# Head of a 15-product matmul kernel: whole-row loads, float16 casts ahead of TensorE's transposes, tile 9 by a transfer

## The chip, the core and the metric

The kernel runs on one core of one Trainium2 chip. The metric is device time in microseconds (us) of one execution; lower is better.

## What is computed

Two matrix products share x; the tanh of the one multiplies the other.

```python
batch, m, k, n = 16, 512, 1024, 768          # x: (16, 512, 1024), w1 and w2: (1024, 768), float32

def reference(x, w1, w2):
    y1 = np.matmul(x, w1)
    y2 = np.matmul(x, w2)
    return (np.tanh(y1) * y2).astype(np.float32)
```

x has 8192 rows, that is 64 tiles of 128 rows; k is eight blocks of 128.

## The kernel before

**Tiles.** All products run in float16 with sums in PSUM. The 2 x 768 output columns are taken as three blocks of 512: `a` is w1's first 512, `b` is w2's first 512, and `G` is the last 256 columns of w1 beside the last 256 of w2. Tiles 0 to 3 (the head) are multiplied in the plain way: for each tile and block one matmul of 128x512 for each of the eight k. Tiles 4 to 63 go in 20 triples. A triple would need 3 tiles x 3 blocks x 8 matmuls; a fast scheme needs 15 products of four matmuls each (`C_OPS`), on sums of x blocks (`A_SUMS`, made by VectorE for each triple, line 506), on sums of w blocks (`B_SUMS`, 11 of them, made once by VectorE at line 496), and on sums of the results (ScalarE copies and VectorE adds). In all there are 88 plain matmuls, 8 for tile 3's block `b` that is held back to the very end (in 16 halves), and 20 x 15 x 4 in the triples: 1296 matmuls of 512 columns.

**Getting operands.** w arrives as float32 in pieces that SP's queue loads in the order of the table `SP_LOADS` (two on ScalarE's queue, `ACT_LOADS`): `a3` is block a of k = 3 (128 rows of 2 KB), `g2` and `h2` are the 256 last columns of w1 and w2 for k = 2 and 3 (256 rows of 1 KB). Each piece is 256 KB and is cast by ScalarE (line 436) or VectorE (line 438) into the float16 array `wh`, whose columns stand in the order a, g, h, b. Head tiles of x come as float32 in halves of 256 KB (`x2.0` is tile 2, k = 0 to 3); TensorE transposes the float32 itself (line 456), and the way out of PSUM casts to float16. Later tiles are loaded by POOL's queue (line 472), which casts on the way. Tiles 4, 5, 6 and 9 (`POOL_LOADS`) are then transposed by TensorE in float16 (line 464), all others by a DMA transpose on SP's queue (line 475). `5.0:a4` means that POOL waits (a one-column copy of `a4`, line 585) until a4 has landed, and then loads tile 5's first half and the entries that follow. ScalarE also sums |x| and |w| for a range check (line 478).

**Order.** Nothing is left to the hardware to order: a planner in the kernel (`Planner`) simulates the engines from a table of costs, due times and margins (`MARGIN`, `MUL_DUE`), and every engine's queue is written in the order of its start times. `PE_HEAD` gives the order of half blocks (`2a0`: tile 2, block a, k = 0 to 3) and of the first triple's products for due times in the head. `WARM` and `FILLERS` are matmuls of a constant (line 850) whose result is unused: three at the start, and others ahead of the operation that is named. Queues run in order, so a late operation holds up all behind it.

Of the kernel before, what the change touches and what calls it, by code (L numbers as in the profile page):

```python
# [78 lines left out]
PE_HEAD = ("0G1 2a0 1G1 0a1 1a1 2b1 2G0 1G0 0b0 p10 0a0 0b1 p7 p6 p12 2G1 "  # L79
           "p9 3G1 p1 1a0 p11 3a1 2a1 0G0 2b0 3G0 p14 1b1 1b0 3a0 p8")  # L80
# [5 lines left out]
MUL_DUE = 0.200  # L86
MARGIN = {"S": 0.773, "B": 0.080, "T": 5.87, "L": 9.71, "early": 0.024}
# [3 lines left out]
FILLERS = {"PT0.1": (256,)}  # L91
# [4 lines left out]
EARLY_LOADS = {0: 0.35}  # L96
# [235 lines left out]
def kernel(  # L332
# [7 lines left out]
    nc = tc.nc  # L340
    P = 128
# [10 lines left out]
    XH_BUFS, XT_BUFS, S_BUFS, O_BUFS, C_BUFS, WF_BUFS = 7, 3, 2, 4, 2, 12  # L352
    D_SLACK, T_SLACK = 10.68, 1.17
    S_SOON, S_FROM, D_FROM, D_EARLY = 6.65, 2, 8, 2.87
    SPLIT = 5
    PACE, STORES, ST_HEAD, ST3G = "4544", (1.56, 2.37, 3.04), (12, 17, 19), 100
    sp_loads = [("Lx" if n[0] == "x" else "L") + n.lstrip("x") for n in SP_LOADS.split()]
    act_loads = ["L" + n for n in ACT_LOADS.split()]
    y_tiles = {int(n[1]) for n in SP_LOADS.split() if n[0] == "y"}
    x32_tiles = {int(n[1]) for n in SP_LOADS.split() if n[0] == "x"}  # L360
    XF_BUFS, XG_BUFS = max(len(x32_tiles), 1), max(HEAD - len(x32_tiles), 1)
# [50 lines left out]
    def load_x32(e, mt, h):  # L412
        if mt not in x32:
            x32[mt] = xfpool.tile([P, K], f32, tag="xf", name="x_f")
        pin(nc.sync.dma_start(x32[mt][:, h * F:(h + 1) * F], xf[mt][:, h * F:(h + 1) * F]))  # L415

    def load_y(e, mt, h):
        wfs[mt, h] = wfpool.tile([P, F], f32, tag="wf", name="w_f")
        pin(nc.sync.dma_start(wfs[mt, h], xf[mt][:, h * F:(h + 1) * F]))

    def cast_y(e, mt, h):
        if mt not in xhs:
            xhs[mt] = xgpool.tile([P, K], f16, tag="xh", name="xh")
        copy(e, xhs[mt][:, h * F:(h + 1) * F], wfs[mt, h])

    def load_w(e, c, k):

        wfs[c, k] = wfpool.tile([P, F], f32, tag="wf", name="w_f")
        if c in "ab":
            pin(engine[e].dma_start(wfs[c, k], wr["ab".index(c)][:, k, :F]))  # L430
        else:
            pin(engine[e].dma_start(wfs[c, k].rearrange("p (k n) -> p k n", k=2), wr["gh".index(c)][:, k:k + 2, F:]))
# [7 lines left out]
    COLUMNS = {"a": 0, "g": F, "h": N, "b": 2 * F}  # L440

    def cast_w(e, c, k):
        lo = COLUMNS[c]
        if c in "ab":
            copy(e, wh[:, k, lo:lo + F], wfs[c, k])
        else:
            copy(e, wh[:, k:k + 2, lo:lo + G], wfs[c, k].rearrange("p (k n) -> p k n", k=2))
# [32 lines left out]
    def abs_x(e, mt):  # L480
        abs_sum(e, x32[mt] if mt in x32 else xhs[mt], mt)
# [4 lines left out]
    def w_block(v):  # L486
        if v in wsum:
            return wsum[v]
        bit = v.bit_length() - 1
        lo = (0, 2 * F, F)[bit % 3]  # L490
        return wh[:, bit // 3 * KH:(bit // 3 + 1) * KH, lo:lo + F]
# [3 lines left out]
    def w_sum(e, v, a, b, how):  # L495
        pin(engine[e].tensor_tensor(wsum[v], w_block(a), w_block(b), OP[how]))  # L496
# [21 lines left out]
    def mm(e, chain, mt, k, c, lo, n):  # L518
        begun[chain] = begun.get(chain, 0) + 1
        pin(nc.tensor.matmul(bank(chain)[:, lo:lo + n], xts[mt][:, k, :], wh[:, k, c + lo:c + lo + n], start=begun[chain] == 1, stop=begun[chain] == KO, skip_group_check=True))  # L520
# [19 lines left out]
    def product(e, i, dst, a, b, begins):  # L540

        for k in range(KH):
            n = F // 2 if i == SPLIT and not begins else F
            for lo in range(0, F, n):
                pin(nc.tensor.matmul(place(i, dst)[:, lo:lo + n], x_operand(i, a)[:, k, :], w_block(b)[:, k, lo:lo + n],  # L545
                                     start=begins and k == 0, stop=k == KH - 1, skip_group_check=True))
# [37 lines left out]
    def gate(e, c, k):  # L584
        pin(nc.gpsimd.tensor_copy(held, wfs[c, k][:, :1]))  # L585
# [4 lines left out]
    DVE_F, DVE_G, DVE_S, DVE_B, DVE_W = (0.60, 0.69), (0.33, 0.42), (0.34, 0.42), (1.16, 1.22), (0.33, 0.42)  # L590
    ACT_F, ACT_G, ACT_W, ACT_D, ACT_AW = (0.50, 0.59), (0.29, 0.38), (0.52, 0.61), (1.06, 1.26), (0.84, 1.04)
# [34 lines left out]
    for _, e, z, n in both:  # L626
        more = EARLY_LOADS.get(z, 0.0) if e == "sp" else 0.2 if z == 0 else 0.0
        issuer[n], last = e, last_on[e]
        last_on[e] = n
        if n[1] == "x":  # L630
            z = n[2:]
            mt, h = (int(v) for v in z.split("."))
            parts.setdefault(mt, []).append((h * KH, KH))
            op(n, {"sp": (0.5, 0.5)}, -100, [], load_x32, mt, h, issued=[last], dma=("sp", 0.67 + more, 1.15, 0.55, 0.084))
            op(f"PT{z}", {"pe": (0.52, 0.52)}, None, [n], transpose_32, mt, h, ("T", mt, h), chains=[("T", mt, h)])
            op(f"T{z}", {"dve": DVE_F, "act": ACT_F}, None, [f"PT{z}"], evacuate_32, mt, h, ("T", mt, h), chains=[("T", mt, h)])
            early.add(f"T{z}")
        elif n[1] == "y":
            z = n[2:]
            mt, h = (int(v) for v in z.split("."))  # L640
            parts.setdefault(mt, []).append((h * KH, KH))
            op(n, {"sp": (0.5, 0.5)}, -100, [], load_y, mt, h, issued=[last], behind=back[-WF_BUFS:][:1] if len(back) >= WF_BUFS else [],
               dma=("sp", 0.67 + more, 1.15, 0.55, 0.084))
            op(f"cy{z}", {"dve": DVE_W, "act": ACT_W}, None, [n], cast_y, mt, h)
            op(f"PT{z}", {"pe": (0.25, 0.25)}, None, [f"cy{z}"], transpose_16, mt, h * KH, KH, ("T", mt, h), chains=[("T", mt, h)])
            op(f"T{z}", {"dve": (0.36, 0.45), "act": (0.51, 0.6)}, None, [f"PT{z}"], evacuate_16, mt, h * KH, KH, ("T", mt, h), chains=[("T", mt, h)])
            early.add(f"T{z}")
            back.append(f"cy{z}")
        else:
            c, k = n[1], int(n[2])  # L650
            op(n, {e: (0.49, 0.49) if e == "sp" else (ISSUE_ACT, 0.5) if n != act_loads[-1] else (ISSUE_ACT + TABLE, 0.5)}, -100, [], load_w, c, k, issued=[last], behind=back[-WF_BUFS:][:1] if len(back) >= WF_BUFS else [],
               dma=(e, (0.67 if c in "ab" else 0.72) + more, 1.15, 0.55, 0.084 if c in "ab" else 0.045))
            op(f"c{c}{k}", {"dve": DVE_W, "act": ACT_W}, None, [n], cast_w, c, k)
            back.append(f"c{c}{k}")
    sp_last = last_on["sp"]
    for t in range(2):
        for k in range(KO):
            op(f"aw{t}{k}", {"act": ACT_AW}, 60 + 10 * (t * KO + k), [f"c{c}{k // 2 * 2 if c in 'gh' else k}" for c in ("ag", "hb")[t]], abs_w, t, k)
    last, xh_order, on_pe = "", [], {}
    for entry in POOL_LOADS.split():  # L660
# [4 lines left out]
        if gated:  # L665
            op(f"gate{z}", {"pool": (0.2, 0.2)}, -100, [f"L{gated}"], gate, gated[0], int(gated[1]), issued=[last])
            last = f"gate{z}"
        if mt >= HEAD and mt not in xh_order:
            xh_order.append(mt)
        op(f"L{z}", {"pool": (0.55, 0.55)}, -100, [], load_x, mt, lo, n, issued=[last], dma=("pool", 0.03 + 1.35 * n / KO, 2.4, 0.55, 0.172 * n / KO))  # L670
# [13 lines left out]
    def loads_of(mt):  # L684
        if mt not in parts:
            return [f"L{mt}"]
        return [("Lx" if mt in x32_tiles else "cy" if mt in y_tiles else "L") + part(mt, k)[1:] for k in (0, KO - 1)]
# [5 lines left out]
    for c, lo in (("a", 0), ("G", F), ("b", 2 * F)):  # L693
        for mt in range(HEAD):
# [4 lines left out]
            for n, k in enumerate(K_ORDER):  # L699
                w = [f"c{c}{k}"] if c != "G" else [f"cg{k // 2 * 2}", f"ch{k // 2 * 2}"]  # L700
                name = f"m{mt}{c}{k}"
                op(name, {"pe": (MM, MM)}, head_at[f"{mt}{c}{k // KH}"] + n % KH * MM, w + [part(mt, k)], mm, chain, mt, k, lo, 0, F, chains=[chain])
                last.append(name)
# [13 lines left out]
    def casts(v):  # L717
        bit = v.bit_length() - 1
        ks = range(bit // 3 * KH, (bit // 3 + 1) * KH)
        return [f"c{c}{k}" for c in ("a", "b", "gh")[bit % 3] for k in ks if c in "ab" or k % 2 == 0]  # L720
# [75 lines left out]
    for h in range(2):  # L796
        chain = ("held", h)
        last = []
        for n, k in enumerate(K_ORDER):
            name = f"m3b{k}{h}"  # L800
            op(name, {"pe": (MM / 2, MM / 2)}, held_at[h] + n * MM / 2, [f"cb{k}", part(HEAD - 1, k)], mm, chain, HEAD - 1, k, 2 * F, h * G, G,
# [7 lines left out]
    for mt in xh_order + [mt for mt in range(HEAD, MT) if mt not in xh_order]:  # L809
        if mt not in parts:  # L810
# [3 lines left out]
            held_for = xh_order[-1 - int(PACE[min(max(mt - 10, 0), len(PACE) - 1)])]  # L814
# [9 lines left out]
    for mt in range(MT):  # L824
# [4 lines left out]
        elif mt >= MT - 3 or mt in (MT - 6, MT - 5, MT - 4):  # L829
# [143 lines left out]
```

## Time and profile before

| what | value |
|---|---|
| median of three runs | 301.74 us (300.5, 301.74, 306.5) |
| the profiled execution's own time | 300.99 us |
| its span in the profile | 299.4 us |
| TensorE (PE) busy | 292.8 us, 98% |
| VectorE (DVE) busy | 252.2 us, 84% |
| ScalarE (ACT) busy | 228.6 us, 76% |
| chain that ended last | PE 88%, DMA 8% |

In the profile's lines the first two numbers are start and duration in us; `xN` counts instructions; PEld is the loading of TensorE's weights, which runs beside matmuls. Matmuls are pipelined: the distance between starts is what one costs, and the duration that is listed is longer. The profiled execution took 1.6 us more than its span, and stands 0.75 us under the median.

### The profile page before, as it was taken

The page shows a single profiled execution, that of the slowest core. Times are in us where ns is not written, and L with a number is a line of the kernel's source. Part 1 is how long each engine was busy: PE and PEld are TensorE (multiplying, and loading weights), DVE is VectorE, ACT ScalarE, POOL GpSimd, SP SyncE. Part 2 cuts the span into 40 slices and gives each one's busy share as a digit, 9 for nine tenths or more (in the row PEclk, how much of TensorE's full clock was granted, in tenths as well). Part 3 has the DMA queues.
Part 4 walks back from the last instruction along what each step waited for, and adds up shares of the span by engine and source line. Part 5 has one row for each costly group of instructions (what it writes and reads, how often), then busy time and mean ns, then how long its engine had stood idle before and what let it go on. Part 6 is the DMA issues. An engine that isn't in the chain of part 4 may idle for free.

```text
span 299.4 us, 4721 instructions
## 1 busy us (share of the span) xinstructions
PE 292.8 (98%) x1421; PEld 138.8 (46%) x1421; DVE 252.2 (84%) x517; ACT 228.6 (76%) x455; POOL 45.9 (15%) x122
## 2 busy tenths in 40 slices
PE   7899999999999999999999999999999999999995
PEld 3544544444444666444444444444444444444443
DVE  1258999999898988989898898988989888899685
ACT  3698999999999968686865869696676957757561
POOL 1007040211202111101021111111201011000000
PEclk9999999999999999999999999999999999999999
DMA  7999999999999999999999999999999999771416
GB/s 222 374 380 266 169 181 183 247 236 194 251 247 232 202 232 258 236 166 252 170 255 235 179 203 202 217 238 223 221 174 260 166 239 198 194 194 52 175 56 212
DMA packets 84091, 64.29 MB, mean 215 GB/s; under 512 B 61792, under 2 KB 65504, under 8 KB 84064
## 3 DMA queue, kind: packets, MB, share of 16 engines
q1 hardware_dynamic: 74720, 47.72, 62.3%
q0 software_dynamic: 8928, 15.73, 34.6%
q10 hardware_dynamic: 416, 0.52, 0.5%
q8 instruction: 11, 0.18, 0.2%
q14 instruction: 16, 0.13, 0.2%
HBM read 39.85 MB, written 25.17 MB: 217 GB/s over the span
## 4 chain that ended last, share of the span: by engine, by line
PE 88%; DMA 8%; POOL 1%; SPq 1%; ACT 0%; issue 0%; DVE 0%
PE bank L545 87%; DMA w_f<-in_w_dram 6%; DMA xh<-in_x_dram 2%; PE bank L520 1%; POOL xh L472 1%; SPq L415 1%; ACT junk L478 0%; PE bank L464 0%; ACT wh L436 0%; POOL held L585 0%; DVE o_last L527 0%; SPq L430 0%; PE bank L576 0%
## 5 line engine op out<-in xcount | busy, mean ns | idle before, releaser
L545 PE MATMUL bank<-b,s 128*128 128x512 f16 (+1 forms) x664 | 148.3, 371 | 0.0
L545 PEld LDWEIGHTS <-s 128*128 128x128 f16 x832 | 81.2, 98 | 91.4 <-issue 0.5
L549 ACT ACTIVATE s<-bank 128x512 f32<-128x512 f32 x100 | 58.3, 596 | 39.3 <-PE bank L545 39.0
L556 DVE TENSOR_TENSOR bank<-bank,s 128x512 f32<-128x512 f32 x100 | 69.4, 697 | 19.4 <-ACT o L559 7.4
L563 DVE TENSOR_TENSOR o<-o,bank 128x512 f32<-128x512 f32 (+1 forms) x120 | 62.8, 547 | 4.7 <-ACT o L559 3.9
L478 ACT ACTIVATE junk<-xh 128x1024 f16<-128x1024 f16 x60 | 63.1, 1052 | 0.2
L545 PEld LDWEIGHTS <-xT 128*128 128x128 f16 x412 | 40.2, 98 | 46.3 <-DVE b L496 0.4
L545 PE MATMUL bank<-b,xT 128*128 128x512 f16 (+1 forms) x252 | 58.5, 369 | 0.0
L559 ACT ACTIVATE o<-bank 128x256 f32<-128x256 f32 (+1 forms) x80 | 33.5, 436 | 12.7 <-DVE bank L556 6.6
L545 PE MATMUL bank<-wh,s 128*128 128x512 f16 (+1 forms) x168 | 41.1, 369 | 0.0
L545 PE MATMUL bank<-wh,xT 128*128 128x512 f16 x160 | 40.7, 379 | 0.0
L582 POOL COPY held_x<-xT 128x1 f16<-128x1 f16 x52 | 11.8, 227 | 165.8 <-DMA xT<-xh 165.7
L472 POOL DMA_DIRECT2D xh<-in_x_dram x62 | 33.1, 535 | 21.2 <-issue 8.1
L506 DVE TENSOR_TENSOR s<-s,xT 128x512 f16<-128x512 f16 x80 | 32.2, 417 | 0.2
L559 ACT ACTIVATE o<-s 128x512 f32<-128x512 f32 x40 | 24.9, 623 | 0.8 <-DVE s L556 0.8
L549 ACT ACTIVATE bank<-bank 128x512 f32<-128x512 f32 x40 | 21.7, 573 | 3.5 <-PE bank L545 2.6
L506 DVE TENSOR_TENSOR s<-xT 128x512 f16<-128x512 f16 x60 | 24.3, 416 | 0.0
L520 PE MATMUL bank<-wh,xT 128*128 128x512 f16 x72 | 18.7, 378 | 0.0
L506 DVE TENSOR_TENSOR s<-xT,s 128x512 f16<-128x512 f16 x40 | 16.7, 417 | 0.0
L556 DVE TENSOR_TENSOR bank<-s,bank 128x512 f32<-128x512 f32 x20 | 13.9, 693 | 2.2 <-PE bank L545 1.2
L556 DVE TENSOR_TENSOR s<-s,bank 128x512 f32<-128x512 f32 x20 | 13.6, 680 | 0.8 <-ACT s L549 0.5
L478 ACT ACTIVATE junk<-wh 128x768 f16<-128x768 f16 x16 | 13.5, 841 | 0.2
(46 smaller groups left out, 127.1 us busy)
## 6 DMA issues: line engine op xcount, KB each, us to landing
out_dram<-o SPq DMA_DIRECT2D x57, 384.0 KB, 4.9
xh<-in_x_dram POOLq DMA_DIRECT2D x58, 256.0 KB, 5.5
w_f<-in_w_dram SPq DMA_DIRECT2D x22, 256.0 KB, 5.6
x_f<-in_x_dram SPq DMA_DIRECT2D x8, 256.0 KB, 6.0
out_dram<-o SPq DMA_DIRECT2D x6, 256.0 KB, 2.0
xT<-xh SPq DMA_TRANSPOSE x56, 5.4
out_dram<-o SPq DMA_DIRECT2D x6, 128.0 KB, 1.8
w_f<-in_w_dram ACTq DMA_DIRECT2D x2, 256.0 KB, 4.6
```

What stands on the lines that cost most here:

```text
L415: pin(nc.sync.dma_start(x32[mt][:, h * F:(h + 1) * F], xf[mt][:, h * F:(h + 1) * F]))
L472: pin(nc.gpsimd.dma_start(xhs[mt][:, lo * P:(lo + n) * P], xf[mt][:, lo * P:(lo + n) * P]))
L478: pin(nc.scalar.activation(junk[:, :src.shape[-1]], src, ACT.Abs, scale=scale, accum_out=sums[:, column:column + 1]))
L506: pin(engine[e].tensor_tensor(ss[i, v], x_operand(i, a), x_operand(i, b), OP[how]))
L520: pin(nc.tensor.matmul(bank(chain)[:, lo:lo + n], xts[mt][:, k, :], wh[:, k, c + lo:c + lo + n], start=begun[chain] == 1, stop=begun[chain ...
L545: pin(nc.tensor.matmul(place(i, dst)[:, lo:lo + n], x_operand(i, a)[:, k, :], w_block(b)[:, k, lo:lo + n], start=begins and k == 0, stop=k ...
L549: pin(nc.scalar.activation(place(i, dst, True), place(i, src), ACT.Copy, scale=float(sign)))
L556: pin(nc.vector.tensor_tensor(d, a, b, ALU.add if signs == (1, 1) else ALU.subtract))
L559: pin(nc.scalar.activation(out_tile(HEAD + 3 * i + r)[:, lo:lo + n], place(i, src)[:, :n], ACT.Tanh, scale=float(sign)))
L563: pin(nc.vector.tensor_tensor(o, o, place(i, src)[:, at:at + n], ALU.mult))
L582: pin(nc.gpsimd.tensor_copy(held_x, xts[mt][:, 0, :1]))
```

## The change

1. **Loads.** x and w come in whole rows: `y0` is tile 0 (128 rows of 4 KB, 512 KB), `u3` is w1's block k = 3 and `v3` is w2's (128 rows of 3 KB, 384 KB). There are 20 loads where there were 32: 18 on SP's queue and two on ScalarE's. `WF_BUFS` goes from 12 buffers of 256 KB to 7 of 384 KB, and the four x tiles share 3 buffers, so the fourth one issued, y2, waits for a cast of an earlier tile.
2. **Casts.** Each head tile is cast whole to float16 (two on VectorE, two on ScalarE) ahead of its transposes, which are then float16 ones. The 16 w pieces are cast in pieces of 768 columns.
3. **Layout.** `wh` holds w1's 768 columns and then w2's, so that block G is read as two stretches of 256 columns (`w_columns`), in matmuls and in sums of w.
4. **Sums.** |x| of the head tiles is summed from the float16 copies; the sums of |w| may no longer start long ahead of their due time (`AW_SOON`).
5. **Tile 9** leaves `POOL_LOADS`: it is loaded in its turn after 7 and 8 and transposed by DMA.
6. **Constants** (fillers) stand at four places: ahead of tile 1's transposes, of the first matmuls of two w pieces, and ahead of tile 2's last transposes.
7. New numbers for due times, margins and the planner's costs, and a new `PE_HEAD`.

```diff
-FILLERS = {"PT0.1": (256,)}
-SP_LOADS = ("a6 x2.0 x0.1 x0.0 x3.0 h2 x2.1 x3.1 g0 h0 a3 h6 a1 g6 x1.0 "
-            "h4 a0 a7 g4 b4 a5 x1.1 b2 a4 b3 b7 b0 b1 b5 b6")
-ACT_LOADS = "a2 g2"
-POOL_LOADS = "5.0:a4 4.1 4.0 6 5.1 9"
+FILLERS = {"PT1.0": (512,), "m1b2": (192,), "m1b7": (256,), "PT2.1": (448,)}
+SP_LOADS = ("y0 y1 v7 u3 y2 u1 v4 u0 v0 "
+            "v1 v3 u2 u4 v5 v6 u6 u5 u7")
+ACT_LOADS = "y3 v2"
+POOL_LOADS = "5.0:v5 4.0 4.1 5.1 6"
...
-    XH_BUFS, XT_BUFS, S_BUFS, O_BUFS, C_BUFS, WF_BUFS = 7, 3, 2, 4, 2, 12
+    XH_BUFS, XT_BUFS, S_BUFS, O_BUFS, C_BUFS, WF_BUFS = 7, 3, 2, 4, 2, 7
...
+    def cast_y(e, mt):
+        xhs[mt] = xgpool.tile([P, K], f16, tag="xh", name="xh")
+        copy(e, xhs[mt], x32[mt])
+
+    def load_w(e, t, k):
+        wfs[t, k] = wfpool.tile([P, N], f32, tag="wf", name="w_f")
+        pin(engine[e].dma_start(wfs[t, k], wr["uv".index(t)][:, k, :]))
...
+    whs = wh.rearrange("p k (t n) -> p k t n", t=2)
+
+    def w_columns(ks, c, lo, n):
+        if c == "G":
+            assert n == F
+            return whs[:, ks, :, F:]
+        lo += N * "ab".index(c)
+        return wh[:, ks, lo:lo + n]
...
     def abs_x(e, mt):
-        abs_sum(e, x32[mt] if mt in x32 else xhs[mt], mt)
+        abs_sum(e, xhs[mt] if mt in xhs else x32[mt], mt)
...
-            op(f"aw{t}{k}", {"act": ACT_AW}, 60 + 10 * (t * KO + k), [f"c{c}{k // 2 * 2 if c in 'gh' else k}" for c in ("ag", "hb")[t]], abs_w, t, k)
+            op(f"aw{t}{k}", {"act": ACT_AW}, 60 + 10 * (t * KO + k), [f"c{'uv'[t]}{k}"], abs_w, t, k, soon=AW_SOON)
```

How the queues stand, at three places. First TensorE's first work (rows that only repeat are left out). Before, the float32 halves `x_f` are transposed as they land; `ones` are the constants, `xT` a transposed tile:

```order
L850 MATMUL bank_79<-ones 128x256
L456 MATMUL bank_77<-ident,x_f 128x128 [waits DMAHW2_49,Pool_49]
L850 MATMUL bank_78<-ones 128x256
L456 MATMUL bank_78<-ident,x_f 128x128 [waits DMAHW4_49]
L520 LDWEIGHTS xT [waits Activation_49]
L520 MATMUL bank_79<-wh,xT 128x512
L456 MATMUL bank_80<-ident,x_f 128x128 [waits DMAHW5_49]
```

In the changed kernel three tiles (0, 3 and 1) are transposed from the float16 copies `xh` ahead of the first matmul of the product:

```order
L857 MATMUL bank_79<-ones 128x256
L463 LDWEIGHTS xh [waits Activation_49]
L463 MATMUL bank_77<-ident_h,xh 128x128 [waits Pool_49]
L463 LDWEIGHTS xh [waits DVE_49]
L857 MATMUL bank_81<-ones 128x512
L522 LDWEIGHTS xT
L522 MATMUL bank_83<-wh,xT 128x512 [waits DVE_49]
L857 MATMUL bank_77<-ones 128x192 [waits Activation_49]
L522 LDWEIGHTS xT [waits Activation_49]
```

The transposes now wait for a cast (ACT or DVE) and no longer for a DMA. Second, ScalarE in the middle of the head, where it casts w pieces (`wh<-w_f`) and sums |x| and |w| (`junk,sums`). Before:

```order
L478 ACTIVATE junk,sums<-wh 128x768 [waits Activation_49]
L436 CAST wh<-w_f 128x2x256 [waits DMAHW1_49]
L436 CAST wh<-w_f 128x512 [waits DMAHW2_49]
L436 CAST wh<-w_f 128x512 [waits DMAHW3_49]
L436 CAST wh<-w_f 128x2x256 [waits DMAHW4_49]
L436 CAST wh<-w_f 128x512 [waits DMAHW5_49]
L436 CAST wh<-w_f 128x512 [waits DMAHW6_49]
L478 ACTIVATE junk,sums<-x_f 128x1024 [waits Activation_49]
```

In the changed kernel (the casts are those of v0, v1, u4, v6, u6 and u5, in this order):

```order
L427 CAST wh<-w_f 128x768 [waits DMAHW2_49]
L427 CAST wh<-w_f 128x768 [waits DMAHW3_49]
L477 ACTIVATE junk,sums<-xh 128x1024 [waits Activation_49]
L477 ACTIVATE junk,sums<-xh 128x1024 [waits DVE_49,Activation_49]
L427 CAST wh<-w_f 128x768 [waits DMAHW6_49]
L477 ACTIVATE junk,sums<-xh 128x1024 [waits DVE_49,Activation_49]
L427 CAST wh<-w_f 128x768 [waits DMAHW0_49]
L427 CAST wh<-w_f 128x768 [waits DMAHW1_49]
L427 CAST wh<-w_f 128x768 [waits DMAHW2_49]
L477 ACTIVATE junk,sums<-xh 128x1024 [waits Activation_49]
```

Three sums of |x| now stand between the casts of the last w pieces. Third, SP's queue after its last loads. Before, the first transfers are those of tiles 7, 8 and 10 (`DMASW` are POOL's loads):

```order
L430 DMA w_f<-in_w_dram 128x512 [waits DMAHW6_49,Activation_49]
L430 DMA w_f<-in_w_dram 128x512 [waits DMAHW7_49,Activation_49]
L475 DMA_TRANSPOSE xT<-xh 128x8x128 [waits DMAHW0_49,DMASW6_49]
L475 DMA_TRANSPOSE xT<-xh 128x8x128 [waits DMAHW1_49,DMASW7_49]
L475 DMA_TRANSPOSE xT<-xh 128x8x128 [waits DMASW0_49,DMAHW2_49,PE_49,Activation_49]
```

In the changed kernel they are those of 7, 8, 9 and 10:

```order
L423 DMA w_f<-in_w_dram 128x768 [waits DMAHW4_49,DVE_49]
L474 DMA_TRANSPOSE xT<-xh 128x8x128 [waits DMASW5_49]
L474 DMA_TRANSPOSE xT<-xh 128x8x128 [waits DMAHW5_49,DMASW6_49]
L474 DMA_TRANSPOSE xT<-xh 128x8x128 [waits DMAHW6_49,DMASW7_49]
L474 DMA_TRANSPOSE xT<-xh 128x8x128 [waits DMAHW7_49,DMASW0_49,PE_49]
```

Tile 9's transfer has moved in as the third, and the eight float16 transposes that TensorE made for it are gone.

More of the change, by code (lines that the diff above doesn't have):

```diff
@@ L626 @@
     for _, e, z, n in both:
[L627 removed]
+        more = EARLY_LOADS.get(z, 0.0) if e == "sp" else 0.6 if z == 0 else 0.0
         issuer[n], last = e, last_on[e]
         last_on[e] = n
[L630 to L648 removed]
```

117 lines of the change are left out of this document (64 added, 53 removed).

## The prediction

> **What bounds the kernel now.** I read the page's first part, then the chain that ended last, then TensorE's timeline and the windows of the head.
>
> ```profile
> PE 292.8 (98%) x1421; PEld 138.8 (46%) x1421; DVE 252.2 (84%) x517; ACT 228.6 (76%) x455; POOL 45.9 (15%) x122
> ...
> 22.70 0.44 POOL held L585
> 23.14 2.32 POOL xh L472 x4
> 25.45 6.45 DMA xh<-in_x_dram
> ...
> 37.54 52.89 PE bank L545 x244
> 90.43 0.03 issue
> 90.46 191.07 PE bank L545 x928
> ...
> 296.28 0.42 DVE o_last L527
> ```
>
> From about 32 us on the chain is TensorE alone, with one step of 0.03 us; before that it is loads: w pieces, then POOL's gate at 22.70 and tiles 4 to 6 behind it. So the time is what TensorE has to do, and how late the loads let it do it.
>
> ```profile
> 120.00:160.00 40.00, 40.00 (x187) 18.12 (x186) 35.46 (x75) 29.23 (x61) 6.43 (x18) 1.00 1.04 211
> ...
> 0.00:27.50 27.50, 16.43 (x69) 6.55 (x69) 1.00 0.99 321
> ```
>
> The first row is a window of the steady part (length, busy time and count of PE, PEld, DVE, ACT, POOL, then clock, DMA share, GB/s): 185 to 187 matmuls of 512 columns in 40 us (one or two straddle an edge), 0.216 us each. The second counts line 520, the head's plain matmuls: 69 have begun by 27.5 us. The head on TensorE:
>
> ```profile
> 1.30 4.64 PE L850 MATMUL bank<-ones 128*128 128x512 f32 x6 [1.30 <-DVE ones L846]
> 6.16 0.63 PE L456 MATMUL bank<-ident,x_f 128*128 128x128 f32 x4 [0.22 <-DMA x_f<-in_x_dram]
> 6.62 0.60 PE L850 MATMUL bank<-ones 128*128 128x256 f32 x2
> ...
> 8.48 0.38 PE L520 MATMUL bank<-wh,xT 128*128 128x512 f16 x1
> ...
> 24.45 3.43 PE L520 MATMUL bank<-wh,xT 128*128 128x512 f16 x15
> 28.57 0.40 PE L464 MATMUL bank<-ident_h,xh 128*128 128x128 f16 x4 [0.69 <-DMA xh<-in_x_dram]
> 28.81 0.81 PE L520 MATMUL bank<-wh,xT 128*128 128x512 f16 x3
> ...
> 31.47 0.38 PE L520 MATMUL bank<-wh,xT 128*128 128x512 f16 x1
> 31.95 0.40 PE L464 MATMUL bank<-ident_h,xh 128*128 128x128 f16 x4
> ...
> 36.93 0.61 PE L464 MATMUL bank<-ident_h,xh 128*128 128x128 f16 x8
> 37.41 2.97 PE L545 MATMUL bank<-b,s 128*128 128x512 f16 x13
> ```
>
> The first product matmul is at 8.48; the 69th ends at 24.45 + 15 x 0.216 = 27.7; TensorE then stands 0.9 us until 28.57, since tile 5's first half lands only then, and 0.27 us more before 31.95. This adds up: after 28.57 there remain 1296 - 69 = 1227 matmuls (264.9 us) and 32 float16 transposes of 0.24 us per four (28.57 to 28.81; 1.9 us), which gives 295.4; the chain leaves TensorE at 296.28. So all waits and restarts after 28.57 come to 0.9 us, and there is nothing to gain but before that.
>
> **The loads.** Before: 24 pieces with rows of 2 KB, 8 with rows of 1 KB, 256 KB each.
>
> ```profile
> 7.96 0.34 SPq L430 DMA_DIRECT2D w_f<-in_w_dram  x1
> ...
> 16.49 5.20 SPq L430 DMA_DIRECT2D w_f<-in_w_dram  x8
> ...
> w_f<-in_w_dram SPq DMA_DIRECT2D x2, 256.0 KB, 5.4
> ...
> 20.00:25.00 5.00, 5.00 (x26) 2.44 (x25) 4.68 (x7) 4.89 (x10) 2.30 (x5) 1.00 1.06 386
> ```
>
> SP issues a load when the one eight places ahead has landed, so the distance of issues is that of landings. The last eight: (5.20 - 0.33)/7 = 0.696 us for 256 KB. From 7.96 to 16.49 there are 12 steps, 0.711 each; five of the pieces that land in them have 1 KB rows, so those take 0.73. Doubling the row saves 0.035 us, mostly a cost per row. Bounds for the new pieces: by bytes alone (a longer row brings nothing) 1.04 us for 384 KB and 1.39 for 512 KB; if each step of length saves another 0.035, 1.0 and 1.33. I take the latter, as the row of the shorter rows points there. Sum before 24 x 0.696 + 8 x 0.73 = 22.5 us, after 16 x 1.0 + 4 x 1.33 = 21.3: 1.2 us less. The last w piece landed at 21.36 + 5.4 = 26.8 (its issue and the second row's time to landing) and would land at 25.6. POOL's gate opens with four w pieces to come, at 21.6 where it was 22.7, so tiles 4 and 5 land 1.1 us earlier.
>
> [...]
>
> **What TensorE loses at the start.** Nearest rows for the new casts:
>
> ```profile
> L436 ACT CAST wh<-w_f x18: 602/617/621, 4.9 to 25.4; 128x512 f16<-128x512 f32 x18
> L438 DVE CAST wh<-w_f x6: 418/426/428, 4.7 to 27.5; 128x512 f16<-128x512 f32 x6
> L478 ACT ACTIVATE junk<-x_f x4: 1048/1054/1057, 21.2 to 33.8; 128x1024 f16<-128x1024 f32 x4
> L478 ACT ACTIVATION_READ_ACCUMULATOR junk<-xh x60: 185/192/237, 33.5 to 270.6; 128x1 f32 x60
> L478 ACT ACTIVATE junk<-wh x16: 834/843/851, 7.3 to 98.9; 128x768 f16<-128x768 f16 x16
> ```
>
> A cast of 768 columns lies between 0.62 and 1.05 us on ACT (I take 0.85, as the sum over 768) and between 0.43 and 0.85 on DVE (0.62); a whole x tile takes 1.05 on ACT and 0.8 on DVE. Counting back from 25.6 in steps of 1.0 and 1.33: y0 and y3 land at 6.7, y1 and v2 at 9.3, v7 10.3, u3 11.3, y2 12.6, u1 13.6, v4 14.6, u0 15.6, v0 16.6, v1 17.6, v3 18.6, u2 19.6, u4 20.6, v5 21.6, v6 22.6, u6 23.6, u5 24.6. y0 is cast by 7.9 and its transposes follow; y1 and v2, both on DVE, are cast by 10.7; so the first product matmul is at 10.75 instead of 8.48. Then TensorE goes in the pace of the casts: four matmuls at 11.95 (behind v7 and u3), three at 14.6 (u1), three at 15.7 (v4), three or four for each of u0, v0 and v1 as they are cast, all gaps short and partly filled by constants. From u2 on a piece serves five matmuls (1.1 us) and TensorE is nearly full. Two waits of 0.3 us remain, for u4 and v6, since ACT has its sums of 1.05 + 0.19 us in front of these casts: v1 is cast by 18.45, two sums until 20.9, u4 by 21.75, a sum until 23.0, v6 by 23.85, u6 24.7, u5 25.55. u7 on DVE is done by 26.6; its six matmuls end at 28.0.
>
> At 28.0 TensorE has then done 64 plain matmuls, where before it had done 69 at 27.7 and stood still until 28.57. The other five take until 29.1: **+0.5 us** against the 28.57 at which it went on before. The eight float32 groups of transposes (0.44 us a group against 0.24) lie in this stretch on both sides, beside waits for loads; their saving is inside the 28.0.
>
> **What comes back.** Tile 9's eight transposes leave TensorE: 36.93 to 37.41, **-0.48 us**. Then the tiles from POOL (its issues, and the time from issue to landing of halves):
>
> ```profile
> 23.08 0.68 POOL L472 DMA_DIRECT2D xh<-in_x_dram  x1
> ...
> 23.75 0.54 POOL L472 DMA_DIRECT2D xh<-in_x_dram  x1
> ...
> 24.27 0.55 POOL L472 DMA_DIRECT2D xh<-in_x_dram  x1
> ...
> xh<-in_x_dram POOLq DMA_DIRECT2D x4, 128.0 KB, 5.4
> ```
>
> Three halves landed at 28.5, 29.1 and 29.7, then tile 6, and the fourth half at 31.9, where TensorE waited for it. Now the four halves go first, 1.1 us earlier: 27.4, 28.0, 28.6 and 29.2. TensorE, at 28.0 with u7, takes tile 4's halves (the second and the third) at 28.0 and 29.1 and tile 5's from 29.5 on, so the stop of 0.27 us goes too: **-0.27**. Late next is tile 6, needed at 30.6 and landing at about 30.8 (31.9, the end of that step of the chain, less 1.1).
>
> Terms at nothing, and their cover. The sums from float16 copies: 1.048 us for 1.054, ACT off the chain. The sums of |w| held back: ACT is 73% busy from 120 us on. y2's buffer: y2 may be issued only when DVE has cast y3, about 7.5 us, and 14 loads stand behind it on SP; but v7 and u3 keep the DMA engines busy until 11.3, so y2 is in time by 2 us; without that cover every load moves with it. Block G in two stretches: 32 matmuls in the head and 80 in the triples. The split triple bounds it:
>
> ```profile
> 80.00:120.00 40.00, 39.97 (x230) 22.28 (x229) 35.71 (x76) 35.28 (x75) 7.35 (x20) 1.00 1.17 236
> ```
>
> Here 44 matmuls of 512 are issued as two of 256, and 230 - 44 = 186 stand in the window as elsewhere; so a second stretch costs at most 0.2/44 us, 0.5 us over 112, and nothing if no address cost exists; I take 0, since 186 is in the range above. Sums of w with a G operand on DVE are not waited for in the chain.
>
> **Sum**: +0.5 - 0.48 - 0.27 = -0.25 us on the profiled execution's 300.99, 300.7 us. That run lay 0.75 us under the median of the three, so against the median it is 0.3%.
>
> **Rivals.**
> - *The loads come a microsecond earlier than my steps* (long rows at less than 1.0 and 1.33, or the first landing before 6.7): all casts and u7 move by it, and TensorE with them, down to what its own work allows: 300.7 - 1.1 = 299.6. For it: the head after 18 us is in the pace of the loads. Against: casts on ACT are nearly back to back (4.89 of 5 us in the window 20 to 25). 0.22.
> - *Long rows bring nothing*: 16 x 1.04 + 4 x 1.39 = 22.2 us, the stream ends 0.9 later than I sum, and TensorE with it: 301.6. For it: only one doubling is seen. 0.13.
> - *Slower: tile 9 by a transfer comes too late.*
>
> ```profile
> 34.64 5.15 SPq L475 DMA_TRANSPOSE xT<-xh  x3
> ...
> xT<-xh SPq DMA_TRANSPOSE x56, 5.4
> ```
>
> Tiles 7, 8 and 9 would land at about 32, 33.3 and 34.6, and the third transfer go out at 35 and land 5.4 later, at 40.4. The first product of triple 1 reads tile 9; 60 matmuls and 24 transposes after 28.0 TensorE is there at 42.4. It decides when the transfer is more than 2 us late; as the three issues before spread over 5.15 us, 4 us late is possible: +2, 302.7. 0.08.
> - *Slower: TensorE's clock falls in the new pauses.* The constants at 1.30 ran at 4.64/2560 = 1.8 ns a column, those at 6.62 at most 1.2 so the start is slow until some microseconds of work are done, although the clock is listed as 1.00. Now TensorE pauses from 5.9 to 7.9 and works in pieces until 14.6. If it fell back to half speed from 10.75 until 17, 18 matmuls and the constants would take twice as long, 5 us, of which pauses absorb 2: 303.7. Against: there is work in each stretch of 2 us. 0.07. [...]
>
> **How the numbers follow.** The forecast, 300.7, has 0.5 (no stretch off by more than 0.7 us); the rivals 0.22, 0.13, 0.08 and 0.07. The range reaches to the fast rival less 1.0 for a still faster stream and the spread of runs, 298.6, and to 303.2, above both 302.7 and the median's offset, without the clock's case. The bounds of 2% (about what a measurement of this kernel can tell from no change, with runs from 300.5 to 306.5) are 295.7 and 307.8: no case reaches them alone. Faster 0.02, same 0.95, slower 0.03 for two slow cases together with a disturbed median.
>
> **What would show it.** Right: the first of the plain matmuls near 10.75 us, the gate's copy near 21.6, last w piece near 25.6, 64 plain matmuls begun by 28, no wait of TensorE for `xh`, and steady windows of 185 to 187. Wrong: a gate later than 22.2 (rows bring nothing), a first plain matmul before 10 (the fast rival), TensorE waiting for `xT<-xh` near 42, matmuls 0.43 us apart between 10 and 17, or steady windows with fewer matmuls, which no term above allows.

## The result and the profile after

The changed kernel takes 299.03 us (median of 10 runs, 298.73 to 301.14) where the kernel before takes 300.50 on the same chip (median of 10, 300.26 to 306.5): ratio 0.9957, 95% interval 0.9937 to 0.9978. That is 1.3 us (0.4%) by the ratio and 1.5 us by the medians, well inside 2%, and five to six times the 0.25 us that was forecast. The profiled execution took 298.88 us, its span is 297.3 us (before 299.4). The profiled execution before, 300.99 us, lies 0.5 us above the median of the ten, so the 2.1 us between the spans are more than the change brings as a rule. The one profile of run 4 further down fell into a slower execution; of it only rows up to 50 us are read, where its clock was full.

First the busy shares, then the chain that ended last (start, us, what), both of the changed kernel:

```profile
PE 290.9 (98%) x1419; PEld 137.7 (46%) x1419; DVE 255.5 (86%) x517; ACT 227.6 (77%) x450; POOL 46.7 (16%) x122
```

```profile
8.41 6.84 DMA w_f<-in_w_dram
...
16.13 5.95 DMA w_f<-in_w_dram
...
22.10 0.84 ACT wh L427
...
22.98 3.40 PE bank L522 x15
26.38 0.39 PE bank L463 x4
...
36.63 242.78 PE bank L550 x1168
...
294.17 0.42 DVE o_last L529
```

POOL's gate and the tiles behind it have left the chain. It now goes from the w pieces, by way of ScalarE's casts (the last one, of u6, at 22.10), into TensorE at 22.98 and stays there. Three rows of VectorE, POOL and TensorE say how the head moved:

```profile
24.12 0.56 DVE L429 CAST wh<-w_f 128x768 f16<-128x768 f32 x1 [0.90 <-DMA w_f<-in_w_dram]
```

```profile
20.17 0.57 POOL L589 COPY held<-w_f 128x1 f32<-128x1 f32 x1 [18.27 <-DMA w_f<-in_w_dram]
```

```profile
6.80 1.07 PE L463 MATMUL bank<-ident_h,xh 128*128 128x128 f16 x16 [1.59 <-ACT xh L427]
...
9.16 0.38 PE L522 MATMUL bank<-wh,xT 128*128 128x512 f16 x1
...
15.79 3.71 PE L522 MATMUL bank<-wh,xT 128*128 128x512 f16 x16
...
26.38 0.40 PE L463 MATMUL bank<-ident_h,xh 128*128 128x128 f16 x4
```

The last w piece landed at 24.1 us, where it was 26.8 before: the loads end 2.7 us sooner, not 1.2. The gate opens at 20.17 (22.70 before), the first plain matmul is at 9.16 (8.48 before). 64 plain matmuls are done at 26.38, so 69 would be at 26.38 + 5 x 0.216 = 27.46, against 28.57 before: 1.1 us gained where 0.5 had been forecast as lost.

From 26.38 on there remain 1232 matmuls (266.0 us at 0.2159) and 24 transposes (1.45 us); that gives 293.8, and TensorE ends at 294.14, just ahead of the chain's last step. The waits after the head thus sum to 0.3 us, where they were 0.9 before. So the span's 2.1 us are 1.1 (the head) + 0.48 (tile 9's transposes) + 0.6 (stops behind the head).

These are the sizes in two executions, and the one before was late in its loads. Run 6 below has the same x and w loads as the kernel before: there the last w piece landed at 26.25 us and TensorE went on at 27.99, where the profile before has 26.77 and 28.57. So some 0.5 us of the 2.7 and of the head's 1.1 can belong to that one execution. The steady part is as before:

```profile
120.00:160.00 40.00, 40.00 (x187) 18.15 (x186) 35.70 (x74) 32.62 (x69) 7.28 (x18) 1.00 1.07 208
```

### The profile page after: what moved, and what is told of

Same layout as the page of the kernel before. It is cut to its first block, busy times and chain, and to the rows that moved or that the text cites. A ratio compares the mean times of both kernels' runs of the same rounds, so it can differ in the third digit from the quotient of the medians.

```text
span 297.3 us, 4698 instructions
## 1 busy us (share of the span) xinstructions
PE 290.9 (98%) x1419; PEld 137.7 (46%) x1419; DVE 255.5 (86%) x517; ACT 227.6 (77%) x450; POOL 46.7 (16%) x122
## 4 chain that ended last, share of the span: by engine, by line
PE 91%; DMA 6%; ACT 1%; SPq 0%; DVE 0%; issue 0%
PE bank L550 87%; DMA w_f<-in_w_dram 4%; PE bank L522 3%; DMA x_f<-in_x_dram 2%; ACT wh L427 1%; PE bank L463 1%; SPq L423 0%; DVE o_last L529 0%; SPq L415 0%; PE bank L580 0%
## 5 line engine op out<-in xcount | busy, mean ns | idle before, releaser
L477 ACT ACTIVATE junk<-xh 128x1024 f16<-128x1024 f16 x64 | 67.3, 1051 | 0.2
L507 DVE TENSOR_TENSOR s<-xT 128x512 f16<-128x512 f16 x60 | 25.0, 418 | 0.0
```

Source lines behind the costliest of these rows:

```text
L477: pin(nc.scalar.activation(junk[:, :src.shape[-1]], src, ACT.Abs, scale=scale, accum_out=sums[:, column:column + 1]))
L507: pin(engine[e].tensor_tensor(ss[i, v], x_operand(i, a), x_operand(i, b), OP[how]))
```

## The theories and the runs

Theory A: the gain is the load stream's; TensorE follows it through the casts until 26.4 us, and tile 9 gives its half microsecond besides. Rival B: it is TensorE's own early work (float16 transposes in place of float32 ones, constants elsewhere). Two more questions stood beside these: whether ScalarE's sums cause the two stops near 20 and 22 us, as the prediction had it, and how much room tile 9's transfer has.

**1. Shorter rows.** The same loads in the same order, each row cut in two (1.5 KB for w, 2 KB for x) by a padded tile:

```diff
-        wfs[t, k] = wfpool.tile([P, N], f32, tag="wf", name="w_f")
-        pin(engine[e].dma_start(wfs[t, k], wr["uv".index(t)][:, k, :]))
+        wfs[t, k] = wfpool.tile([P, 2, N // 2 + 8], f32, tag="wf", name="w_f")[:, :, :N // 2]
+        pin(engine[e].dma_start(wfs[t, k], wr["uv".index(t)][:, k, :].rearrange("p (h n) -> p h n", h=2)))
...
```

> The changed kernel with each load's rows cut in two on the way into SBUF (1.5 KB for w, 2 KB for x); same bytes, same 20 loads, same order of every queue. Theory A (the gain comes from the load stream, which long rows make faster and so earlier): by the steps before, 0.696 us per 256 KB with 2 KB rows and 0.73 with 1 KB, a w piece takes 1.07 us and an x tile 1.39, against 0.98 and 1.30 in the changed kernel; the last w piece lands 1.8 us later, at about 25.9, and the time is 1.3 to 1.8 us above the changed kernel's 299.0, so about that of the kernel before (ratio 0.999 to 1.002). Theory B (the gain is TensorE time saved on transposes: 8 groups at 0.44 against 0.24 us, 1.6 us, and tile 9's 0.48, together 2.1): no difference, 299.0, ratio 0.995.

Measured: 300.20 us, ratio to the kernel before 0.9982 (0.9963 to 1.0001), span 298.7. Its last w piece (VectorE's row), and two windows each of before, of this run and of the changed kernel (the last column is GB/s):

```profile
25.57 0.70 DVE L428 CAST wh<-w_f 128x768 f16<-128x768 f32 x1 [1.03 <-DMA w_f<-in_w_dram]
```

```profile
2.00:8.00 6.00, 5.00 (x13) 2.05 (x11) 0.85 (x2) 2.99 (x4) 0.00 (x0) 1.00 1.00 306
10.00:20.00 10.00, 9.66 (x48) 4.67 (x48) 3.37 (x5) 8.23 (x15) 0.00 (x0) 1.00 1.07 372
```

```profile
2.00:8.00 6.00, 4.51 (x20) 2.13 (x19) 0.81 (x2) 2.67 (x3) 0.00 (x0) 1.00 0.95 351
10.00:20.00 10.00, 9.78 (x48) 4.55 (x47) 2.86 (x6) 8.18 (x11) 0.00 (x0) 1.00 1.06 381
```

```profile
2.00:8.00 6.00, 4.41 (x23) 2.36 (x22) 1.17 (x3) 3.00 (x4) 0.00 (x0) 1.00 0.97 365
10.00:20.00 10.00, 9.87 (x49) 4.57 (x48) 3.58 (x6) 8.47 (x13) 0.00 (x0) 1.00 1.03 401
```

The stream ends 1.45 us later and the span is 1.4 us longer (1.2 us by the medians, taken on two chips): TensorE follows the loads about one for one. A holds. The 1.45 us have two parts. From y2's landing on, the 13 w pieces took 1.035 us each (12.09 to 25.55) where the changed kernel's took 0.982 (11.32 to 24.09): 0.7 us, the length of the rows. The other 0.77 us were there when y2 landed. In that stretch a second thing is mixed in: a load with twice the rows also takes longer to issue on SP (two w loads in 1.67 us, where they took 1.20), and how much of the 0.77 is the issue is not shown.

**2. Float32 transposes again.** The same loads; x is not cast, and TensorE transposes the float32:

```diff
-SP_LOADS = ("y0 y1 v7 u3 y2 u1 v4 u0 v0 "
+SP_LOADS = ("x0 x1 v7 u3 x2 u1 v4 u0 v0 "
...
-ACT_LOADS = "y3 v2"
+ACT_LOADS = "x3 v2"
...
```

> The changed kernel with the same loads, but TensorE transposes the head tiles in float32 as before, without the casts ahead. Theory A: the transposes lie where TensorE waits for loads, and each tile is there a cast earlier; nothing to 0.3 us slower, 299.0 to 299.3, ratio 0.995 to 0.996, and the first product matmul up to 0.9 us earlier than 9.16. Theory B: 8 groups at 0.2 us more, 1.6 us slower, 300.6, ratio 1.000.

Measured: 299.34 us, 0.9960 (0.9944 to 0.9976), span 298.0: 0.3 us over the changed kernel by the medians, 0.7 by the spans. TensorE's rows of this run:

```profile
6.10 2.27 PE L455 MATMUL bank<-ident,x_f 128*128 128x128 f32 x16 [0.16 <-DMA x_f<-in_x_dram]
...
26.77 0.39 PE L463 MATMUL bank<-ident_h,xh 128*128 128x128 f16 x4
```

The transposes take twice as long (2.27 us for the 1.07 of the changed kernel), but start 0.7 us sooner and fall into time in which TensorE waits for w anyway; at 26.77 it is 0.4 us behind. B, which asked for 1.6 us, falls: the casts are worth some 0.3 us, at most the 0.7 of the spans.

**3. No constants in the early pauses.**

```diff
-FILLERS = {"PT1.0": (512,), "m1b2": (192,), "m1b7": (256,), "PT2.1": (448,)}
+FILLERS = {}
```

> The changed kernel without the four constants in the early pauses; nothing else moves. Theory A: the constants fill pauses, so nothing to 0.2 us faster, 298.8 to 299.0, ratio 0.995. Theory C (the constants keep TensorE's clock up): the matmuls between 9 and 14 us start 0.43 us apart instead of 0.216, and the time is 1 to 3 us longer, 300 to 302.

Measured: 299.16 us, 0.9953 (0.9936 to 0.9969). The constants are worth nothing that can be measured; the theory in which they keep TensorE's clock up, with 1 to 3 us more without them, falls. The profiled execution (span 298.5) did show something else, tile 9's transfer too late; its waits from 30 to 50 us, and behind them the same wait in the changed kernel:

```profile
PE bank L550 <- DMA xT<-xh: 1.0, 1, 1.0
```

```profile
PEld L550 <- DMA xT<-xh: 0.2, 1, 0.2
```

There only a weight load waited: the transfer landed at 40.62 us, 0.2 us ahead of the matmul at 40.82 that uses it. Without the constants it landed at 41.90, and TensorE stood for 1.15 us.

**4. Tile 9 back on TensorE.**

```diff
-POOL_LOADS = "5.0:v5 4.0 4.1 5.1 6"
+POOL_LOADS = "5.0:v5 4.0 4.1 5.1 6 9"
```

> The changed kernel with tile 9 put back on TensorE's transposes (eight of them, 0.45 to 0.48 us, at about 36 us where TensorE waits for nothing). Theories A and B alike: 0.4 to 0.6 us slower, 299.4 to 299.6, ratio 0.9965. A rival, that the transfer of tile 9 holds up what is behind it on SP's queue: no slower or faster, 299.0 or less.

Measured: 300.49 us, 1.0004 (0.9979 to 1.0030): 1.5 us more, three times the transposes' own time. The planner also laid VectorE's and ScalarE's work out anew. The stretch from 30 to 50 us, here and in the changed kernel:

```profile
30.00:50.00 20.00, 19.42 (x95) 8.71 (x93) 19.53 (x37) 17.08 (x33) 4.60 (x11) 1.00 1.18 190
```

```profile
30.00:50.00 20.00, 20.00 (x94) 8.96 (x93) 19.73 (x37) 17.91 (x34) 4.26 (x9) 1.00 1.23 172
```

VectorE is busy 19.7 of 20 us there. With tile 9 on TensorE, TensorE idles for 0.6 us in this window by its busy time, and by the distances of its matmuls' starts it has four stops of 0.26 to 0.34 us, 1.2 us in all, that end with these rows:

```profile
37.12 2.76 PE L550 MATMUL bank<-b,s 128*128 128x512 f16 x12
40.04 1.02 PE L550 MATMUL bank<-b,s 128*128 128x512 f16 x4 [0.17 <-ACT s L553]
...
42.88 1.02 PE L550 MATMUL bank<-b,xT 128*128 128x512 f16 x4
...
45.82 1.02 PE L550 MATMUL bank<-wh,xT 128*128 128x512 f16 x4 [0.18 <-DVE o L567]
```

The changed kernel has none of them. The trace puts two of them down to waits for ScalarE and VectorE.

**5. Eight more transposes, nothing else.** To price the transposes without a new plan, tile 6's are issued twice:

```diff
-        for k in range(lo, lo + n):
+        for k in [*range(lo, lo + n)] * (2 if mt == 6 else 1):
```

> The changed kernel with tile 6's eight float16 transposes issued a second time (the second set writes the same banks with the same values; only TensorE gets eight more instructions, the other engines' orders are those of the changed kernel). It asks what tile 9's eight transposes cost TensorE when nothing else is replanned. Theory A (a transpose costs its own slot, about 0.06 us, and the 1.46 us that tile 9 back on TensorE had cost came mostly from the VectorE and ScalarE orders that were planned anew with it): 0.45 us more than the changed kernel, 299.5, ratio to the kernel before about 0.997. Rival B (transposes among the steady matmuls cost more than their slot, as the whole 1.46 us lies with them): 300.4 or more, ratio about 1.000.

Measured: 299.21 us, 0.9960 (0.9936 to 0.9984), 0.24 us over the changed kernel in the same session (run 11), span 0.4 us over it. In TensorE's timeline the group grew from 0.61 to 1.06 us:

```profile
29.02 1.06 PE L463 MATMUL bank<-ident_h,xh 128*128 128x128 f16 x16
```

So eight transposes cost between 0.24 us (the medians) and 0.45 us (their row), and not the 1.5 of run 4. The other microsecond there fits the four stops, 1.2 us, that came with the new plan.

**6. Tile 9 by a transfer, alone.** The kernel before with only that part of the change:

```diff
-POOL_LOADS = "5.0:a4 4.1 4.0 6 5.1 9"
+POOL_LOADS = "5.0:a4 4.1 4.0 6 5.1"
...
-            held_for = xh_order[-1 - int(PACE[min(max(mt - 10, 0), len(PACE) - 1)])]
+            held_for = xh_order[-1 - int(PACE[min(mt - 10, len(PACE) - 1)])] if mt >= 10 else mt
```

> The kernel before with one part of the change alone: tile 9 loaded after 7 and 8 and transposed by DMA. By TensorE's work alone: 0.48 us faster, 300.0, ratio 0.9984. The rival (the third transfer is the late one): tile 9 lands at 41 us or later, TensorE waits for it before triple 1's first product, and the gain is lost, 300.4 to 302, ratio 1.000 or more. In the changed kernel's trace it landed 0.2 us ahead of its use.

Measured: 301.59 us, 1.0037 (1.0023 to 1.0051): slower. TensorE's stops in it:

```profile
36.82 3.61 PE L545 MATMUL bank<-b,s 128*128 128x512 f16 x16 [0.58 <-DVE s L556]
...
51.99 1.89 PE L545 MATMUL bank<-b,xT 128*128 128x512 f16 x8 [0.22 <-ACT bank L549]
...
59.44 1.02 PE L545 MATMUL bank<-wh,xT 128*128 128x512 f16 x4 [0.38 <-ACT o L559]
```

The transposes' 0.48 us are saved and more is lost in these three stops, which the trace puts down to VectorE and ScalarE, as in run 4. The rival's number came true, but its cause only in part: tile 9's transfer was late, at 42.05 us, but held TensorE up by only 0.1 us (until 42.10), because the stop that ends at 36.82 had delayed TensorE already. Whether the part has its gain with the change's own due times alone was not tried.

**7. ScalarE's sums held back.** The sums of |x| may start 4 us later, so that the casts of u4 and v6 have nothing ahead of them:

```diff
-        op(f"D{mt}", {"act": ACT_D}, ORIGIN - 8 + 4.33 * mt, loads_of(mt), abs_x, mt, slack=12.0)
+        op(f"D{mt}", {"act": ACT_D}, ORIGIN - 8 + 4.33 * mt, loads_of(mt), abs_x, mt, slack=16.0)
```

> The changed kernel with the sums of |x| of the head tiles held back 4 us more, so that ScalarE casts all w pieces first (order of the later work changes a little too). Theory A: the two stops of TensorE near 20.4 and 22.5 us (0.25 and 0.29) go, 0.3 to 0.6 us faster, 298.4 to 298.7, ratio 0.993 to 0.9945. Theory B: no difference, 299.0; later sums could also push ScalarE's work after 25 us and cost something, 299.0 to 299.6.

Measured: 303.22 us, 1.0090 (1.0068 to 1.0112). The expectation was wrong in both theories. In the changed kernel ScalarE casts u4 and v6 as they land; the sum ahead ends just then (ScalarE's rows):

```profile
19.21 0.82 ACT L427 CAST wh<-w_f 128x768 f16<-128x768 f32 x1
...
20.89 0.19 ACT L477 ACTIVATION_READ_ACCUMULATOR junk<-xh 128x1 f32 x1
21.13 0.83 ACT L427 CAST wh<-w_f 128x768 f16<-128x768 f32 x1
```

The sum's last instruction ends at 21.08 and v6 landed at 21.11. Nor are these the pieces that TensorE waits for. Its two stops end at 20.76 and 22.98; the casts that end just ahead are those of v5, on VectorE (the row below), and of u6, on ScalarE (22.10 in the chain above), and both began within 0.03 us of the landing (20.12 and 22.08):

```profile
20.14 0.56 DVE L429 CAST wh<-w_f 128x768 f16<-128x768 f32 x1
```

With the sums out of the way TensorE's stops between 18 and 24 us sum to about 0.55 us as in the changed kernel, and larger ones appear where the sums went (TensorE's rows of this run, the stop for u6 and the two largest):

```profile
22.89 0.59 PE L522 MATMUL bank<-wh,xT 128*128 128x512 f16 x2 [0.16 <-ACT wh L427]
...
37.29 1.46 PE L522 MATMUL bank<-wh,xT 128*128 128x512 f16 x6 [1.65 <-ACT o L525]
...
45.56 1.02 PE L550 MATMUL bank<-b,xT 128*128 128x512 f16 x4 [1.13 <-DVE s L507]
```

The two stops of 0.25 and 0.29 us in the changed kernel are the loads' pace, not the sums.

**8. Four more matmuls among the steady ones.** In triple 10, each of the four products that begin a bank of sums issues its first matmul twice:

```diff
-            for to, w in parts:
+            for to, w in parts * (2 if begins and k == 0 and i == 10 else 1):
```

> The changed kernel with the same four matmuls added in triple 10 (about 165 us), where TensorE waits for nothing. Theories A and B alike: 0.86 us slower, 299.9, ratio 0.9985. It gives the price of a matmul away from the head, and so of tile 9's transposes.

Measured: 300.06 us, 0.9983 (0.9968 to 0.9997), span 298.7: 1.0 us over the changed kernel's 299.03. The chain has one long stretch of steady matmuls:

```profile
37.15 243.64 PE bank L550 x1172
```

The changed kernel's began at 36.63 and took 242.78 us with 1168 matmuls. So the four cost 0.86 us, 4 x 0.216: in the dense part a matmul costs its slot. The other 0.52 us of this longer span are a slower start, taken up at the end.

**9. Four more matmuls at 9 to 12 us**, in two runs of the same kernel:

```diff
+        for _ in range(2 if begun[chain] == 1 and chain in (("b", 1), ("b", 0), ("a", 1), ("a", 0)) else 1):
```

> The changed kernel with the first matmul of four early groups (blocks b and a of tiles 0 and 1, between 9 and 12 us) issued twice, four matmuls or 0.86 us more of TensorE's work, whose first results are overwritten; nothing else moves. Theory A (the head goes in the pace of the loads, TensorE waits there): 0 to 0.3 us slower, 299.0 to 299.3, ratio 0.995 to 0.996. Theory B (TensorE's work counts everywhere, so cheaper transposes gave the gain): 0.86 us slower, 299.9, ratio 0.998.

> The same kernel as in the run with four more matmuls at 9 to 12 us, for a second profile. There one w piece landed at 24.6 us in place of 23.1 and cost about 1.3 us. Theory A (TensorE has about 1.2 us of gaps between 13 and 26.4 us, so that 0.86 us more of early work is absorbed; the late piece was that one execution's): the piece lands near 23.1 again, the time is 0 to 0.3 us over the changed kernel's. Rival (the work that is added early is not absorbed, or the late piece belongs to this order): again about 1 us over it, ratio to the kernel before near 0.998.

Measured: 300.06 us, 0.9978 (0.9959 to 0.9997), and 299.93, 0.9980 (0.9954 to 1.0005); spans 298.7 and 298.6. The number of theory B (299.9) came true in both, and in the second so did the rival's late piece; but the microsecond is not lost where the four stand. TensorE in the second profile:

```profile
21.61 1.96 PE L523 MATMUL bank<-wh,xT 128*128 128x512 f16 x7
...
25.47 0.59 PE L523 MATMUL bank<-wh,xT 128*128 128x512 f16 x2 [1.26 <-ACT wh L427]
```

```profile
24.59 0.83 ACT L427 CAST wh<-w_f 128x768 f16<-128x768 f32 x1 [1.67 <-DMA w_f<-in_w_dram]
```

At 21.61 TensorE is where it was without them (21.62): the early work is absorbed. Then u5 lands at 24.57 us in place of 23.10, in both profiles, though it was issued at the same time. By the records of the 16 DMA engines, 15 parts of it are there at 23.07 and the last one 1.5 us later. What that engine did stands in the transfers' view from 22 to 23.3 us (packets, MB, share of 16 engines):

```profile
q1 hardware_dynamic: 177, 0.48, 94.0%
q8 instruction: 1, 0.02, 5.3%
```

One packet of 16 KB of the instruction queue took 5.3% of 16 x 1.3 = 1.1 us there. In the changed kernel's same window there is no such row; its packet starts at 23.50. The whole program has 11 packets in this queue, 0.18 MB; TensorE has 1419 matmuls and as many weight loads, 258 for each packet, and in the changed kernel's trace the next packet comes 123 matmuls after the first. So they are most likely TensorE's instructions, which is an estimate from these counts; by it TensorE, with more work early, reaches the place that calls for them a microsecond sooner (the two windows below), while w is still coming in. In none of the other profiles of the changed kernel and its variants does the packet come ahead of u5's landing, and in none of them is u5 late (in the changed kernel's it landed at 23.10, 0.4 us before the packet starts). The two windows (of this run and of the changed kernel) end where the packet starts, and TensorE has begun 98 matmuls in both:

```profile
0.00:22.41 22.41, 20.32 (x98) 10.03 (x99) 8.65 (x15) 15.47 (x22) 3.23 (x12) 1.00 0.92 359
```

```profile
0.00:23.50 23.50, 20.28 (x98) 9.81 (x99) 9.45 (x15) 16.35 (x23) 4.32 (x14) 1.00 0.93 358
```

**10. The same, without the constants**, so that TensorE does not get there sooner (the edits of 3 and 9 together):

> The kernel with four more matmuls at 9 to 12 us, and with the four matmuls on constants that stand in the early pauses left out, so that TensorE has as many instructions before the gate as in the changed kernel. In both profiles with the four more, a 16 KB transfer of the instruction queue held one of the 16 DMA engines for 1.1 us from 22.4 us on, while a w piece still had to pass: it landed at 24.6 us in place of 23.1. In the changed kernel's profiles the same transfer starts at 23.3 to 23.5 us, in all of them when TensorE has begun its 97th or 98th matmul (with the four more: the 98th, which then comes 1 us sooner). Theory F (the late piece comes from this fetch of TensorE's instructions, whose moment goes by the number of its instructions): the fetch starts at 23.3 us or later, the piece lands near 23.1, the last one near 24.1, and the span is 297.3 to 297.8 plus a wait for tile 9's transfer where there is one (it was 1.15 us without the constants); 299.0 to 300.0. Rival (the early work itself is not absorbed, or the late piece has another cause): the piece lands near 24.6 again, and TensorE's 69 plain matmuls are done 1.3 us later than in the changed kernel.

Measured: 298.77 us, 0.9930 (0.9907 to 0.9953), span 297.2. u5's cast on ScalarE and TensorE at the end of the head:

```profile
23.09 0.83 ACT L427 CAST wh<-w_f 128x768 f16<-128x768 f32 x1 [0.16 <-DMA w_f<-in_w_dram]
```

```profile
26.31 0.40 PE L463 MATMUL bank<-ident_h,xh 128*128 128x128 f16 x4
```

The packet starts at 23.44, u5 is on time, TensorE is at 26.31 where the changed kernel is at 26.38, and nothing waits for tile 9. The four matmuls cost nothing. The fetch theory holds in what it said of time: no early packet, no late piece. Its count does not hold exactly. The trace lists each constant as two matmuls, so TensorE has four fewer here than in the changed kernel, not as many; the packet starts with 94 begun (106 in run 3's profile, where it came at 26.38). What sets its moment is not shown. At 298.77 against the changed kernel's 298.97 on the same chip this kernel is not shown to be faster: the two ratios' intervals overlap.

**11. The changed kernel once more.**

> The changed kernel once more, unedited, for a second profile and more times. If the gain is the loads' pace: ratio to the kernel before near 0.9957, the last w piece lands within 0.5 us of 24.1 us, and 69 plain matmuls are done within 0.5 us of 27.5 us. Open is whether TensorE waits for tile 9's transfer: it came 0.2 us ahead of need in the first profile and about 1 us late in that of the kernel without the constants' early places. If it is late here too, the span is 298 to 298.5 in place of 297.3.

Measured: 298.97 us, 0.9954 (0.9939 to 0.9970), span 297.2; the last w piece at 24.0, and no wait for tile 9 this time.

## Why the prediction was right in sign and small in size

**The step that failed** is "Sum before 24 x 0.696 + 8 x 0.73 = 22.5 us, after 16 x 1.0 + 4 x 1.33 = 21.3: 1.2 us less", with the counting back from 25.6 that rests on it. The mechanism held (the loads end sooner, and TensorE follows them); the size did not: the last w piece landed at 24.1, 1.5 us earlier than counted. Two terms are behind it.

- The steps, 0.4 us: a w piece took 0.982 us for the 1.0 and y2 1.30 for the 1.33, so the stream is 16 x 0.982 + 4 x 1.30 = 20.9 us, as are 8.39 MB at the 401 GB/s of the window. The price of the row's length was nearly right: in run 1, where the row is half as long, a w piece took 1.035 us for the 0.982, that is 0.053 us for 384 KB or 0.035 for 256 KB, the figure that was carried over. That it is mostly a cost per row was the author's estimate and is not shown: 128 rows fewer saved 0.035 us there and 0.053 here.
- The start, 1.1 us: the sum kept it where it was (26.8 - 22.5 = 4.3 us), as a term that it did not name, and it came to 24.1 - 20.9 = 3.2. The first two x tiles landed at 5.67 and 5.87 us, where the counting back has 6.7 (and 7.0 by its own steps, 9.3 - 1.33 - 1.0).

From 2 to 8 us 365 GB/s moved where 306 did, which is 354 KB or 0.9 us. Run 1 had 351 GB/s there with rows of 1.5 and 2 KB, so most of this is not the length of the rows; fewer and larger loads and their order are left, and were not taken apart. Part of it was the one profile that the sum was read from: in run 6, with the loads of before, the same window has 318 GB/s, and the start comes to 26.25 - 22.5 = 3.8.

**What hung on it**: the first plain matmul (9.16 for 10.75), the gate (20.17 for 21.6), and +0.5 at 28.57, which became -1.1. This is the rival in which the loads come a microsecond earlier than the steps; it gave 299.6, and it had named a first plain matmul before 10 as its sign. Its limit, TensorE's own work, was not reached: runs 9 and 10 show that the early head still has room for 0.86 us. What the new order of the matmuls and the new due times (item 7 of the change) gave by themselves, no run takes apart.

**A cause that was wrong without harm**: two stops of 0.3 us are there, but they stand behind the landings of v5 and u6 (run 7), not behind u4 and v6 and ScalarE's sums.

**Right**: tile 9's transposes, -0.48 (run 5: 0.24 to 0.45). The stop before 31.95 is gone; with smaller ones it gave 0.6 for the 0.27 named, in the two profiled executions. Sums from float16, block G in two stretches, y2's buffer: nothing of them is seen, and the steady window has 187 matmuls.

**The other rivals.** *Long rows bring nothing* falls with 401 GB/s against 372 and 381 from 10 to 20 us (the windows of run 1). *Tile 9's transfer too late* was nearer than its 0.08: a margin of 0.2 us in one profile, a wait of about a microsecond in another (run 3), none in a third. The transfer landed as forecast, at 40.6 us for 40.4; it was TensorE that came earlier, at 40.8 for 42.4. *The clock falls in the pauses* did not happen: between 10 and 17 us no matmuls of the changed kernel stand at twice the distance (its products start 0.215 to 0.233 us apart where one follows another), though TensorE had paused for 1.59 us before 6.80.

## What to carry to other kernels

When a load stream sets a head, sum its start and its rate apart, and read both from windows in GB/s, of more than one execution if there are any; here the start moved by 1.1 us between the two profiles, which a sum of steady steps cannot show. Before an edit is priced by the instructions that it removes, look whether the engines beside it have any room: here VectorE is 98 to 99% busy from 30 to 50 us, and two edits worth half a microsecond lost one or more when the order there was planned anew. Work that is put into a pause can move something else that is keyed to progress into a busy stretch: here, most likely, a fetch of instructions through the same DMA engines; the four matmuls cost 1.0 us in run 9, where it came early, and nothing in run 10.

## What the runs showed of the hardware

One 16 KB packet of the instruction queue held one of the 16 DMA engines for 1.1 us, and in both profiles in which it came ahead of a load that is spread over all 16, that load landed 1.5 us late (run 9). Without the early packet the load was on time (run 10).

The time at which TensorE came to its full pace differed between two profiled executions of the same start. These are TensorE's first rows in the changed kernel and in run 8, with the same six constants and the same 16 transposes:

```profile
1.30 3.92 PE L857 MATMUL bank<-ones 128*128 128x512 f32 x6 [1.30 <-DVE ones L853]
6.80 1.07 PE L463 MATMUL bank<-ident_h,xh 128*128 128x128 f16 x16 [1.59 <-ACT xh L427]
```

```profile
1.30 4.63 PE L857 MATMUL bank<-ones 128*128 128x512 f32 x6 [1.30 <-DVE ones L853]
6.70 1.89 PE L463 MATMUL bank<-ident_h,xh 128*128 128x128 f16 x16 [0.77 <-ACT xh L427]
```

In run 8 the transposes start 0.107 us apart, twice the 0.055 of the changed kernel, although the granted clock is listed as 1.00 in both. By the distances of starts the change came at 10.8 us in run 8; in the changed kernel it came between 4.02 and 4.62 us, the starts of the fourth and the fifth constant, which are 0.86 us apart in run 8. Run 8's constants took 4.63 us, a pause of 0.77 us followed, and the transposes from 6.70 on were still slow; what sets the moment of the change, no run shows. The late rise can have cost run 8 no more than the 0.52 us at the end of its head, since TensorE waits for loads in much of that stretch; whether it is the whole cause of them was not tried.
